# A routing table spread by one-hot products: the scaling moved from VectorE to ScalarE, one turn ahead

## The chip, the cores and the metric

The kernel runs on one core of a Trainium2 chip. Its engines work in parallel, each through its own queue in order: TensorE (PE, with its weight loads as PEld), VectorE (DVE), ScalarE (ACT), GpSimd (POOL) and SyncE (SP), which issues the DMAs. The metric is the device time of one execution in microseconds; the runs of a kernel are given by their median.

## The reference, cut to what matters

The program is a network of two blocks with two layers each, for 256 tokens of 1024 channels. The change sits in the second block, in a feed-forward part that chooses among 16384 experts for each token and head:

```python
s1, s2 = <q1, sub_keys[0]>, <q2, sub_keys[1]>        # 128 + 128 key scores, 8 heads
v1, i1 = top_k(s1, 16);  v2, i2 = top_k(s2, 16)
top_s, pos = top_k(v1[:, None] + v2[None, :], 16)    # 16 of 256 pairs
expert = i1 * 128 + i2 (at pos);  g = softmax(top_s)
w = g * gelu(u_tab[expert] @ h);  y = sum of w * v_tab[expert]
```

Layer 0 does this for 256 tokens and for 256 context tokens, layer 1 for the 256 tokens alone.

## The kernel before

Instead of gathering experts, the kernel computes all of them. `hidden` (L1088) takes one block of 128 experts, loads its weights, cuts them in a high and a low part (`split`: ACT casts the high part on L198, DVE subtracts it on L199), multiplies them with the tokens on PE (three products each, L232 to L234, 48 for 512 tokens, 24 for 256) and applies a gelu on ACT (L1104). `ahead` runs 128 such expert blocks for layer 0 and 126 for layer 1; the result goes to memory. Afterwards `experts` reads it back, weights it with a dense table G of factors [expert, token] and multiplies with the second table.

G is made beside `ahead`, in two steps for each group of 128 tokens. `choose` finds the 16 pairs of each head and leaves a tile R with four columns for each token: first index k0, second index k1, and the factor in a coarse and a fine part, g0 and g1. `spread` turns R into G: per token it makes a one-hot of k0 and two one-hots of k1 scaled by g0 and g1, 128x128 each in 16 bits, for the 128 choices of the token; PE multiplies the first with the second and third and adds up (two products, L1061). Four tokens are one turn: 12 instructions of DVE (L1056 once and L1058 twice for each token), 8 products, one copy from PSUM by ACT (L1062). A group has 32 turns, and after every fourth turn 1 MB of G is stored. The tile E of a turn comes from the tag "wb", a ring of three buffers that weights of other parts use too.

How these steps mix is given by a plan (P0 for layer 0, P1 for layer 1, L39 and L40): pairs of a start and a rate, in units of 256 tokens of expert blocks. Each unit advances each active generator by its rate. In layer 0 a block of 512 tokens counts as two units, and the four spreadings run at 0.8 to 0.95 turns per unit, one after the other, most of the time beside a `choose`. In layer 1 the first spreading runs at 0.5 turns per unit from unit 45 on, the second at 0.85 from unit 85 on, so that for some 25 units both run. The framework then sets the final order of instructions on each engine with its own estimate of their readiness, so that a cast for a later block can stand ahead of a gelu of an earlier one. Two pairs of buffers hold the split weights ("ws", four tiles): a cast for the block after the next can begin when PE has finished the present block.

Below, "block 1" is this stretch of layer 0 (1285 to 1872 us) and "block 2" that of layer 1 (2945 to 3234 us); an "expert block" is one call of `hidden`, and a "turn" is four tokens of a spreading.

Of the kernel before, what the change touches and what calls it, by code (L numbers as in the profile page):

```python
# [12 lines left out]
F16 = mybir.dt.float16  # L13
U32 = mybir.dt.uint32
AF = mybir.ActivationFunctionType
ALU = mybir.AluOpType
AX = mybir.AxisListType

P = 128
# [5 lines left out]
NT = 16  # L25
GSCALE = 2.0 ** 14
# [27 lines left out]
class Net:  # L54
# [989 lines left out]
    def spread(self, r, Gd, nb):  # L1044


        nc = self.nc
        for q in range(P // NT):
            st = self.t("k8", [P, P, NT])
            for m in range(0, NT, 4):  # L1050
                n = q * NT + m
                pG = self.p("C", [P, 4, P])
                E = self.t("wb", [P, 4, 3, P], F16)
                for j in range(4):
                    k0, k1, g0, g1 = (r[:, i, n + j:n + j + 1] for i in range(4))
                    nc.vector.tensor_scalar(E[:, j, 0], self.iota16, k0, None, ALU.is_equal)  # L1056
                    for i, g in enumerate((g0, g1)):
                        nc.vector.tensor_scalar(E[:, j, 1 + i], self.iota16, k1, g, ALU.is_equal, ALU.mult)  # L1058
                for j in range(4):
                    for i in range(2):  # L1060
                        nc.tensor.matmul(pG[:, j], E[:, j, 0], E[:, j, 1 + i], start=i == 0, stop=i == 1)  # L1061
                nc.scalar.activation(st[:, :, m:m + 4], pG.rearrange("p n e -> p e n"), AF.Copy, scale=1 / GSCALE)  # L1062
                if m == NT - 4:
                    nc.sync.dma_start(Gd[:, nb + q], st)
                yield

    def routing(self, l, hs, Gd, order, early, plan):

        ss = [self.t("k8", [P, 16, P]) for _ in range(2 * len(hs))]
        R = {}

        def choose(i):
            R[i] = yield from self.choose(self.rt, ss[i])

        def spread(gen, i, nb):
            self.done(gen)
            yield from self.spread(R[i], Gd, nb)

        gens = [choose(i) for i, _ in order]
        for _ in self.key_scores(l, hs, ss):
            for g in gens[:early]:
                next(g), next(g)
        gens += [spread(g, *o) for g, o in zip(gens, order)]
        return [(t, g, r) for g, (t, r) in zip(gens, plan)]
# [324 lines left out]
```

## Time and profile before

| | us |
|---|---|
| median of 3 runs | 3605.29 (3605.12 to 3605.36) |
| profiled execution | 3616.49 |
| its span | 3614.7 |
| PE busy in the span | 3506.5 (97%) |
| DVE busy | 2563.6 (71%) |
| ACT busy | 1520.0 (42%) |
| L1056 and L1058, DVE | x768 and x1536, mean 246 and 307 ns |

The page gives shares of the whole span; stages differ. A busy PE is not one at its peak, since the ends of matmuls are modelled, so pace is better read from the starts of equal instructions, an expert block's gelu for example. Instructions of ACT and DVE also overlap a little at their ends, so that two in a row take less than twice the duration of one.

### The profile page before, as it was taken

To read this page: it belongs to the slowest core of one execution; us is meant where nothing else is said; L and a number is where in the kernel's file an instruction comes from. 1 tells how busy PE (TensorE), PEld (TensorE's weight loads), DVE (VectorE), ACT (ScalarE), POOL (GpSimd) and SP (SyncE) were. 2 spreads that over 40 slices of the span, in tenths; PEclk is the share of its full clock that TensorE was granted. 3 is DMA by queue.
4 is the path that set the end of the run, shared out by engine and by line. 5 is a ranking of instruction groups with operands and counts; after the bars stand their busy time and mean duration, and the time that the engine had idled before them with its cause. 6 is when DMAs were issued, how large, how long until landed. Compare 5 with 4: busy or idle time off the path is not lost.

```text
span 3614.7 us, 59733 instructions
## 1 busy us (share of the span) xinstructions
PE 3506.5 (97%) x22400; PEld 3053.3 (84%) x22400; DVE 2563.6 (71%) x6767; ACT 1520.0 (42%) x2555; POOL 51.9 (1%) x72
## 2 busy tenths in 40 slices
PE   8999989999999999999999999999999999999999
PEld 6677777899899999998997888888878999888877
DVE  6666776655753799999777655554476789987666
ACT  5533455544553433333333222222254545455443
POOL 1000010000000000000000000000000000000000
PEclk9999999999999999999999999999999999999999
DMA  6555644566522754454579877776223677788986
GB/s 220 168 175 199 209 153 131 184 202 201 167 94 82 223 183 166 163 174 175 181 246 295 263 249 237 236 226 188 76 72 110 214 234 239 240 275 293 291 259 197
DMA packets 329394, 712.85 MB, mean 197 GB/s; under 512 B 28304, under 2 KB 170256, under 8 KB 322704
## 3 DMA queue, kind: packets, MB, share of 16 engines
q1 hardware_dynamic: 329104, 709.05, 60.5%
q8 instruction: 175, 2.87, 0.3%
q14 instruction: 115, 0.94, 0.1%
HBM read 606.44 MB, written 102.50 MB: 196 GB/s over the span
## 4 chain that ended last, share of the span: by engine, by line
PE 67%; DVE 21%; DMA 8%; issue 1%; ACT 1%; SPq 1%; POOL 0%; DVEq 0%; POOLq 0%; ACTq 0%
PE psC L233 9%; PE psC L234 9%; PE psC L232 9%; PE psA L234 8%; PE psA L232 8%; PE psA L233 8%; DVE wb L1058 6%; DVE ws L199 4%; DMA wb<-in_v 3%; DMA k<-kept 3%; PE psB L233 3%; PE psB L232 3%; PE psB L234 3%; DVE wb L1056 2%; DVE k L199 2%; DMA wb<-in_ada_w 1%
## 5 line engine op out<-in xcount | busy, mean ns | idle before, releaser
L198 ACT CAST ws<-w 128x1024 fp32r<-128x1024 f32 (+1 forms) x528 | 547.6, 1037 | 923.5 <-PE psA L233 626.1
L199 DVE TENSOR_TENSOR ws<-w,ws 128x1024 fp32r<-128x1024 f32 (+1 forms) x528 | 635.6, 1205 | 366.4 <-ACT ws L198 360.9
L234 PE MATMUL psA<-b,ws 128*128 128x256 f32 x2760 | 784.2, 284 | 29.3 <-DVE ws L199 28.2
L232 PE MATMUL psA<-b,ws 128*128 128x256 f32 x2760 | 787.4, 285 | 1.1 <-ACT ws L198 1.1
L233 PE MATMUL psA<-b,ws 128*128 128x256 f32 x2760 | 776.6, 281 | 0.0
L234 PEld LDWEIGHTS psA<-b,ws 128*128 128x128 f32 x2760 | 521.8, 189 | 43.7 <-DVE ws L199 43.1
L232 PEld LDWEIGHTS psA<-b,ws 128*128 128x128 f32 x2760 | 522.3, 189 | 7.0 <-ACT ws L198 3.6
L233 PEld LDWEIGHTS psA<-b,ws 128*128 128x128 f32 x2760 | 522.6, 189 | 0.2
L234 PE MATMUL psC<-k,k 128*128 128x512 f32 x1056 | 416.3, 395 | 7.0 <-DVE k L199 6.9
L232 PE MATMUL psC<-k,k 128*128 128x512 f32 x1056 | 417.1, 395 | 6.0 <-ACT k L198 6.0
L233 PE MATMUL psC<-k,k 128*128 128x512 f32 x1056 | 416.4, 394 | 0.0
L1058 DVE TENSOR_SCALAR wb<-iota,R 128x128 f16<-128x128 f16 x1536 | 413.3, 307 | 0.0
L199 DVE TENSOR_TENSOR k<-wb,k 128x1024 fp32r<-128x1024 f32 x256 | 312.4, 1220 | 60.8 <-ACT k L198 60.6
L198 ACT CAST k<-wb 128x1024 fp32r<-128x1024 f32 x256 | 268.4, 1050 | 199.4 <-DMA wb<-in_v 199.1
L198 ACT CAST k<-k 128x256 fp32r<-128x256 f32 (+1 forms) x272 | 137.3, 506 | 484.0 <-PE psA L234 422.6
L1151 DVE TENSOR_TENSOR k<-k,b 128x256 f32<-128x256 f32 x384 | 149.9, 421 | 211.7 <-DMA k<-kept 209.7
L234 PEld LDWEIGHTS psC<-k,k 128*128 128x128 f32 x1056 | 198.5, 188 | 60.3 <-DVE k L199 15.0
L233 PE MATMUL psC<-ws,k 128*128 128x512 f32 (+1 forms) x608 | 240.5, 396 | 5.7 <-DVE ws L199 4.6
L232 PEld LDWEIGHTS psC<-k,k 128*128 128x128 f32 x1056 | 198.9, 188 | 52.6 <-ACT k L198 8.1
L232 PE MATMUL psC<-ws,k 128*128 128x512 f32 (+1 forms) x608 | 239.7, 398 | 0.6 <-ACT k L198 0.2
L234 PE MATMUL psC<-ws,k 128*128 128x512 f32 (+1 forms) x608 | 238.0, 392 | 0.0
L233 PEld LDWEIGHTS psC<-k,k 128*128 128x128 f32 x1056 | 199.0, 188 | 44.2
(400 smaller groups left out, 6250.0 us busy)
## 6 DMA issues: line engine op xcount, KB each, us to landing
w<-in_u SPq DMA_DIRECT2D x256, 512.0 KB, 4.3
wb<-in_v SPq DMA_DIRECT2D x256, 512.0 KB, 4.5
w<-in_w_ff SPq DMA_DIRECT2D x128, 512.0 KB, 4.5
G<-k SPq DMA_DIRECT2D x48, 1024.0 KB, 6.1
b<-G SPq DMA_DIRECT2D x48, 1024.0 KB, 8.5
wb<-in_ada_w SPq DMA_DIRECT2D x80, 512.0 KB, 4.7
k<-kept SPq DMA_DIRECT2D x128, 256.0 KB, 3.8
w<-in_wA SPq DMA_DIRECT2D x48, 512.0 KB, 4.7
```

The costliest lines, as they stand in the source:

```text
L198: self.nc.scalar.copy(hi, src)
L199: self.nc.vector.tensor_sub(lo, src, hi.bitcast(F32))
L232: self.nc.tensor.matmul(out, ah, bh, start=first, stop=False)
L233: self.nc.tensor.matmul(out, ah, bl, start=False, stop=False)
L234: self.nc.tensor.matmul(out, al, bh, start=False, stop=last)
L1056: nc.vector.tensor_scalar(E[:, j, 0], self.iota16, k0, None, ALU.is_equal)
L1058: nc.vector.tensor_scalar(E[:, j, 1 + i], self.iota16, k1, g, ALU.is_equal, ALU.mult)
L1151: nc.vector.tensor_mul(g3, g3, Gs[i][:, :, j])
```

## The change

DVE now writes the two plain one-hots only (L1055 in the new numbering, twice for each token). ACT makes the two scaled ones from the one-hot of k1 (L1057, a copy with a column of R as scale). Both are issued by a helper `ones` for the turn that follows: in each turn the one-hots of the next come first, then this turn's eight products (L1070), its copy (L1071) and the store. The generator has one step more (33 instead of 32), since the first only prepares. The tile E has four planes for each token instead of three; its tag and ring stay. The gelu is now L1114.

```diff
-        for q in range(P // NT):
-            st = self.t("k8", [P, P, NT])
-            for m in range(0, NT, 4):
-                n = q * NT + m
-                pG = self.p("C", [P, 4, P])
-                E = self.t("wb", [P, 4, 3, P], F16)
-                for j in range(4):
-                    k0, k1, g0, g1 = (r[:, i, n + j:n + j + 1] for i in range(4))
-                    nc.vector.tensor_scalar(E[:, j, 0], self.iota16, k0, None, ALU.is_equal)
-                    for i, g in enumerate((g0, g1)):
-                        nc.vector.tensor_scalar(E[:, j, 1 + i], self.iota16, k1, g, ALU.is_equal, ALU.mult)
...
+        def ones(n):
+            E = self.t("wb", [P, 4, 4, P], F16)
+            for j in range(4):
+                col = [r[:, i, n + j:n + j + 1] for i in range(4)]
+                for i in (1, 0):
+                    nc.vector.tensor_scalar(E[:, j, i], self.iota16, col[i], None, ALU.is_equal)
+                for i in (2, 3):
+                    nc.scalar.activation(E[:, j, i], E[:, j, 1], AF.Copy, scale=col[i])
+            return E
+
+        E = ones(0)
+        yield
+        for n in range(0, P, 4):
+            q, m = divmod(n, NT)
+            nxt = ones(n + 4) if n + 4 < P else None
...
+                    nc.tensor.matmul(pG[:, j], E[:, j, 0], E[:, j, 2 + i], start=i == 0, stop=i == 1)
...
+            E = nxt
+            yield
```

On ACT in block 1, one expert block with two turns read before as follows (ws: high part of split weights; psA: an expert block's product, its number a little above that of its ws; psC: a turn's product; k: results).

```order
L1104 ACTIVATE k_2296_13381<-psA_13332 128x512
L1062 ACTIVATE k_2278_13186<-psC_13390 128x128x4
L1062 ACTIVATE k_2301_13420<-psC_13421 128x128x4
L198 CAST ws_13678<-w_13676 128x1024
L1104 ACTIVATE k_2308_13499<-psA_13450 128x512
```

The same place after the change (wb: the tile E of a turn, R: the columns of factors):

```order
L1114 ACTIVATE k_2295_13415<-psA_13366 128x512
L1071 ACTIVATE k_2286_13316<-psC_13441 128x128x4
L1071 ACTIVATE k_2286_13316<-psC_13474 128x128x4
L1057 ACTIVATE wb_13549<-wb_13549,R_12605 128x128 x8
L1057 ACTIVATE wb_13583<-wb_13583,R_12605 128x128 x8
L198 CAST ws_13612<-w_13610 128x1024
L1114 ACTIVATE k_2306_13540<-psA_13491 128x512
```

Sixteen scalings stand between a gelu and the next cast. Before, the cast ahead of the gelu of psA_13450 was that of ws_13678, the second block behind it (13562 is the first); now the cast ahead of the gelu of psA_13491 is that of ws_13612, the first behind it.

On ACT in block 2, where both spreadings run, before:

```order
L1104 ACTIVATE k_4770_32895<-psA_32870 128x256
L1062 ACTIVATE k_4754_32760<-psC_32898 128x128x4
L198 CAST ws_33038<-w_33036 128x1024
L1104 ACTIVATE k_4777_32952<-psA_32927 128x256
L1062 ACTIVATE k_4744_32678<-psC_32955 128x128x4
L198 CAST ws_33120<-w_33118 128x1024
```

And after:

```order
L1114 ACTIVATE k_4741_33290<-psA_33265 128x256
L1057 ACTIVATE wb_33321<-wb_33321,R_32531 128x128 x4
L1071 ACTIVATE k_4728_33187<-psC_33338 128x128x4
L198 CAST ws_33350<-w_33348 128x1024
L1057 ACTIVATE wb_33382<-wb_33382,R_32531 128x128 x8
L1071 ACTIVATE k_4728_33187<-psC_33399 128x128x4
L198 CAST ws_33412<-w_33410 128x1024
L1057 ACTIVATE wb_33444<-wb_33444,R_30373 128x128 x2
L1114 ACTIVATE k_4750_33379<-psA_33354 128x256
```

The cast of ws_33350, for the very next product psA_33354, now stands behind the gelu of psA_33265, the product ahead of it, and behind four scalings and a turn's copy.

On DVE in block 1, around the subtraction of an expert block (iota: the numbers 0 to 127 that the columns of R are compared with), the queue read before:

```order
L1056 TENSOR_SCALAR wb_13538<-iota_223,R_12605 128x128
L1058 TENSOR_SCALAR wb_13538<-iota_223,R_12605 128x128 x2
L199 TENSOR_TENSOR ws_13563<-w_13560,ws_13562 128x1024
L1056 TENSOR_SCALAR wb_13623<-iota_223,R_12605 128x128
L1058 TENSOR_SCALAR wb_13623<-iota_223,R_12605 128x128 x2
```

And after:

```order
L937 MAX_INDEX k_2229_12705<-k_2229_12705,k_2288_13327 128x8
L1055 TENSOR_SCALAR wb_13424<-iota_223,R_12605 128x128 x5
L1055 TENSOR_SCALAR wb_13457<-iota_223,R_12605 128x128 x8
L199 TENSOR_TENSOR ws_13488<-w_13485,ws_13487 128x1024
L935 MATCH_REPLACE k_2296_13418<-k_2229_12705,k_1889_10059 128x128
```

Eight short instructions stand where twelve stood for a turn, and those of the next turn are issued ahead of the subtraction.

## Rows read from the trace of the kernel before

**Rows 1.** Busy time by engine in five stretches: start:end, length, then busy us (instructions) per engine

```profile
1285.00:1419.00 134.00, 127.95 (x1161) 122.97 (x1160) 134.00 (x616) 43.89 (x70) 0.00 (x0) 1.00 0.51 170
1438.00:1716.00 278.00, 261.27 (x2355) 253.67 (x2354) 269.97 (x1187) 96.89 (x151) 0.00 (x0) 0.98 0.50 170
1744.00:1872.00 128.00, 123.21 (x1118) 117.78 (x1117) 111.74 (x402) 47.73 (x72) 0.00 (x0) 1.00 0.64 221
2945.00:3083.00 138.00, 136.37 (x1214) 133.17 (x1213) 135.74 (x483) 70.77 (x113) 0.00 (x0) 1.00 0.75 245
3084.00:3195.00 111.00, 103.07 (x913) 94.52 (x913) 111.00 (x424) 52.90 (x87) 0.00 (x0) 1.00 0.70 237
```

**Rows 2.** The same stretches, casts of L198 alone on ACT: one (x) per expert block

```profile
1285.00:1419.00 134.00, 18.89 (x19) 1.00 0.51 170
1438.00:1716.00 278.00, 40.28 (x39) 0.98 0.50 170
1744.00:1872.00 128.00, 18.52 (x18) 1.00 0.64 221
2945.00:3083.00 138.00, 44.66 (x43) 1.00 0.75 245
3084.00:3195.00 111.00, 27.68 (x27) 1.00 0.70 237
```

**Rows 3.** The same stretches, copies of L1062 alone on ACT: one (x) per turn

```profile
1285.00:1419.00 134.00, 17.78 (x32) 1.00 0.51 170
1438.00:1716.00 278.00, 35.45 (x64) 0.98 0.50 170
1744.00:1872.00 128.00, 17.82 (x32) 1.00 0.64 221
2945.00:3083.00 138.00, 12.91 (x22) 1.00 0.75 245
3084.00:3195.00 111.00, 19.54 (x34) 1.00 0.70 237
```

**Rows 4.** Timeline of ACT, block 1: start us, us, engine, line, operation [idle before]

```profile
1865.66 0.59 ACT L1104 ACTIVATE k<-psA 128x512 f32<-128x512 f32 x1
1866.15 1.07 ACT L1062 ACTIVATE k<-psC 128x512 f32<-128x512 f32 x2
1871.31 1.05 ACT L198 CAST ws<-w 128x1024 fp32r<-128x1024 f32 x1 [4.08 <-PE psA L233]
1872.26 0.59 ACT L1104 ACTIVATE k<-psA 128x512 f32<-128x512 f32 x1
...
1877.89 0.59 ACT L1104 ACTIVATE k<-psA 128x512 f32<-128x512 f32 x1
```

**Rows 5.** Timeline of ACT, block 2, one spreading at work

```profile
3205.51 0.38 ACT L1104 ACTIVATE k<-psA 128x256 f32<-128x256 f32 x1
3205.78 0.59 ACT L1062 ACTIVATE k<-psC 128x512 f32<-128x512 f32 x1
...
3208.88 0.37 ACT L1104 ACTIVATE k<-psA 128x256 f32<-128x256 f32 x1
```

**Rows 6.** Waits in block 1, 1285 to 1872 us: us in total, times, longest

```profile
PE psA L234 <- DVE ws L199: 20.9, 30, 2.3
```

**Rows 7.** Costliest groups of the page: busy us, mean ns; idle before it

```profile
L199 DVE TENSOR_TENSOR ws<-w,ws 128x1024 fp32r<-128x1024 f32 (+1 forms) x528 | 635.6, 1205 | 366.4 <-ACT ws L198 360.9
```

**Rows 8.** Timeline of DVE inside one turn of the spreading

```profile
1380.26 0.24 DVE L1056 TENSOR_SCALAR wb<-iota,R 128x128 f16<-128x128 f16 x1
1380.42 0.52 DVE L1058 TENSOR_SCALAR wb<-iota,R 128x128 f16<-128x128 f16 x2
1380.87 0.24 DVE L1056 TENSOR_SCALAR wb<-iota,R 128x128 f16<-128x128 f16 x1
```

**Rows 9.** ACT's copies by a column of factors, L845: all twenty, ns min/median/max

```profile
L845 ACT ACTIVATE k<-k,rsrf x20: 385/396/489, 950.9 to 2686.0; 128x128 f32<-128x128 f32 x20
```

**Rows 10.** Timeline of ACT: two of those L845 instructions back to back

```profile
2669.48 0.69 ACT L845 ACTIVATE k<-k,rsrf 128x128 f32<-128x128 f32 x2 [0.60 <-DVE k L842]
```

More of the change, by code (lines that the diff above doesn't have):

```diff
@@ L1047, in spread @@
         nc = self.nc
-        for q in range(P // NT):
-            st = self.t("k8", [P, P, NT])
-            for m in range(0, NT, 4):
-                n = q * NT + m
-                pG = self.p("C", [P, 4, P])
-                E = self.t("wb", [P, 4, 3, P], F16)
-                for j in range(4):
-                    k0, k1, g0, g1 = (r[:, i, n + j:n + j + 1] for i in range(4))
-                    nc.vector.tensor_scalar(E[:, j, 0], self.iota16, k0, None, ALU.is_equal)
-                    for i, g in enumerate((g0, g1)):
-                        nc.vector.tensor_scalar(E[:, j, 1 + i], self.iota16, k1, g, ALU.is_equal, ALU.mult)
[L1059 to L1065, printed above, removed]
+        st = None
+        def ones(n):
[12 more added lines that the diff above has]
+            nxt = ones(n + 4) if n + 4 < P else None
+            if m == 0:
+                st = self.t("k8", [P, P, NT])
+            pG = self.p("C", [P, 4, P])
+            for j in range(4):
+                for i in range(2):
+                    nc.tensor.matmul(pG[:, j], E[:, j, 0], E[:, j, 2 + i], start=i == 0, stop=i == 1)
+            nc.scalar.activation(st[:, :, m:m + 4], pG.rearrange("p n e -> p e n"), AF.Copy, scale=1 / GSCALE)
+            if m == NT - 4:
+                nc.sync.dma_start(Gd[:, nb + q], st)
+            E = nxt
+            yield
     def routing(self, l, hs, Gd, order, early, plan):
```

## The prediction, made before the changed kernel ran

> **What bounds the kernel now.** I first read the page's shares by slice: PE is busy nearly throughout, so only the stretches in which it waits can shorten. These are the ones in which the spreading runs. The busy times by engine there [rows 1] are to be read against two counts, the casts of expert blocks [rows 2] and the copies of turns [rows 3]; together they give each engine's load. The first and the last stretch have DVE busy all of their 134 and 111 us, the second 269.97 of 278; PE is not full in any, and ACT has two thirds free in block 1 and half in block 2. The list of waits says what PE lacks: the low part of split weights, which DVE subtracts, 20.9 us in 30 waits in block 1 [rows 6]. So DVE ends last, by its own work, and the change does shorten that work. The question is what ACT's work then does.
>
> PE's own pace comes from gelu starts [rows 4]: 1877.89 less 1872.26 is 5.63 us for an expert block without a turn, 1872.26 less 1865.66 is 6.60 with two, so a turn costs PE 0.485. In block 2 a block has half as many products, 2.82, and with one turn takes 3.37 (3208.88 less 3205.51 [rows 5]): 0.55 for a turn. With 19, 39, 18, 43 and 27 expert blocks and 32, 64, 32, 22 and 34 turns, PE's work in the five stretches is 122.5, 250.6, 116.9, 133.4 and 94.8 us, against 134, 278, 128, 138 and 111 that pass. What PE could win back is thus 11, 27, 11, 5 and 16 us, 70 in all, some 2% of the run.
>
> **What leaves DVE.** A token's three instructions repeat every 0.61 us (1380.87 less 1380.26 [rows 8]); the plain one starts the next 0.16 later, so each scaled one holds the queue for 0.225. A turn is 4 x 0.61 = 2.44 us. After the change it is 8 x 0.16 = 1.28. DVE gives up 1.16 us for each of 192 turns, 223 us; in the fifth stretch its load falls from 111 to about 72, in the second from 270 to 196. DVE is then no one's bound.
>
> **What ACT takes on.** There are 1536 scalings, 8 for each turn. The kernel has the same operation elsewhere, a 128x128 copy with a column as factor: 0.396 us alone [rows 9], and two in a row 0.69 [rows 10], so the second begins 0.295 after the first. I take 0.295, the nearer row, since the eight of a turn stand one behind the other and only the first of each pair waits for DVE; 0.396 is the other end. Below 0.295 lies what the 16-bit tile might save, of which no row speaks. The Trainium skill, page "ScalarE: Activation LUTs", section "What ACT_TABLE_LOAD costs", gives the same rate per element for fp32 and bf16, 93 ns more for each pointer operand, and 93 ns of overlap between neighbours; worked out for 128 columns that is an estimate of 0.386 alone and 0.293 in a row, so by the page nothing is saved by the 16 bits. No run here shows it yet.
>
> The rest of ACT's work in steps from start to start: a cast 0.95 (1872.26 less 1871.31), a gelu 0.49 (1866.15 less 1865.66), a turn's copy 0.48 (two take 1.07 at 0.59 each) [rows 4]; in block 2 a gelu 0.27 [rows 5]. A turn costs ACT 0.48 + 8 x 0.295 = 2.84, an expert block 1.44 in block 1 and 1.22 in block 2. ACT's load becomes 19 x 1.44 + 32 x 2.84 = 118 us in the first stretch, then 238, 117, 115 and 129.5. In block 1 that is PE's own work to within 5% in all three stretches. In the fifth it is 129.5 where 111 pass today: there the wall moves from DVE to ACT and grows by 18.
>
> **How near a stretch comes to its dearest engine.** Before, a stretch with one clear bound reached it fully (first and fifth) or to 97% (second); the third, where DVE is busy for 87% of the time and PE's work is 91% of it, reached neither. After the change block 1 has PE and ACT level, each in order, each waiting for the other. I take 95% there, between the two, 97% for the fourth stretch and 98% for the fifth:
>
> - first: 122.5 / 0.95 = 129, gain 5; second: 250.6 / 0.95 = 264, gain 14; third: 117 / 0.95 = 123, of which I count 2 and not 5, because there the tag "wb" also serves other weights, whose loads start later when a tile E is held a turn longer;
> - fourth: 133.4 / 0.97 = 137.5, nothing;
> - fifth: 129.5 / 0.98 = 132, loss 21;
> - behind it some ten blocks with 0.85 turns each: ACT 1.22 + 0.85 x 2.84 = 3.63 against PE's 2.82 + 0.85 x 0.55 = 3.29 for each, loss 3;
> - one step more for each group: the last gates of layer 1 are stored one block later at most, 2.82 us, and the stage that reads them follows closely; loss 2.
>
> The products (L1070) and stores keep their number, so PE and SP gain and lose nothing in work. Being a turn ahead hides the new hop from DVE to ACT: a turn's chain of 1.28 and 2.4 us fits in the 6 us between its place and that of its products in block 1; without that cover PE would wait some 3 us per block. The sum is -21 in block 1 and +26 in block 2 with its end: +5 us on a profiled execution of 3616.49, which stands 11 above the median of the runs. A few microseconds scale with that by nothing, so the median goes from 3605.29 to **3610 us**. Its own range, for 92 to 97% in block 1, is 3599 to 3623.
>
> **The rivals.**
>
> *The two loads interlock without loss.* Split weights lie two blocks ahead, so ACT may lag in a block with two turns and catch up in one with one. For it speaks that DVE alone managed 100% in two stretches; against it that the new order puts the cast behind sixteen scalings. At 98% in block 1 the gains are 9, 22 and 9, the fourth stretch gives 2, and the fifth, at just ACT's load, loses 18, its end 5: -19, or 3586 us.
>
> *ACT's queue delays the split, slower.* After a gelu, ACT has two copies (0.96) and sixteen scalings (4.72) ahead of the cast; with gelu and cast (0.49 + 0.95) and DVE's subtraction (1.205 [rows 7]) the low part is ready 8.3 us after PE finished a block, while PE reaches the need for it after two turns and one block, 6.6 us. That is 1.7 us late, if nothing catches up. If half of the 76 blocks in the three stretches pay it, 65 us come on top of PE's 490, 555 against today's 540: +15 instead of -21, and with block 2 at +26, +41. It decides from the point where some 30 blocks pay (490 + 30 x 1.7 is today's 540): from there block 1 gives nothing against block 2's loss. I price it a little lower, at +30, 3635 us, because blocks with a single turn recover. Against it speaks that PE's wait also slows what ACT waits for, so that lags do not add up.
>
> A rule points the same way: the Trainium skill, same page, section "Rules for kernel authors", says to use VectorE and not ScalarE for a multiplication. The rows bear it out for a single instruction, 0.225 on DVE against 0.295 on ACT. By that rule alone the change would lose wherever ACT is level with the bound, which is this rival; what speaks for the change is only that DVE was full.
>
> *The scalings do not overlap.* If each holds ACT for 0.396, a turn costs 3.65 and the five stretches 144, 290, 143, 133 and 157 on ACT: +10, +12, +15, 0 and +46, and 8 more behind: some +90, 3695 us. The pair [rows 10] speaks against it.
>
> That the change does less than it says can be excluded: the scaled one-hots are gone from DVE's queue.
>
> **How the numbers follow.** The forecast has 0.44, the interlocked case 0.30, the delayed split 0.20, the scalings without overlap 0.06. Two tenths of a per cent, 7 us, are about what a measurement of this kernel tells from no change. The interlocked case is almost wholly faster, and of the forecast's spread 0.06 lies below 3598 once its tails are counted: 0.36 faster. About half of the forecast's weight, 0.23, is the same; its upper part, 0.15, and the two last cases make 0.41 slower. For 8 in 10 the range goes from 3572, where block 1 gains 35 and block 2 loses little, to 3640, a little over the delayed split.
>
> **What would show it.** Right: L1057 starting every 0.29 to 0.30 us within a turn; DVE's busy time in the first stretch well under 100% and ACT's over 90% in the first, second and fifth; the first three stretches shorter together by about 20 us, the fifth longer by about 20; waits of PE put down to ACT's scaled one-hots and casts instead of the subtraction behind a full DVE. Wrong: the fifth stretch not longer, which would mean that a turn costs ACT less than 2.4 us; or block 1 unchanged with both engines under 90%, which would be the chains and not the loads.

## The result, and the profile after

The changed kernel took 3645.03 us, the median of four runs (3641.28 to 3657.42), against 3605.32 for the kernel before: a ratio of 1.0109, with a 95% interval of 1.0079 to 1.0139. It is slower by 1.1%, where 3610 had been forecast and 3640 was the upper end. The profiled execution took 3646.82 us, 30 more than that of before. Two single runs, one of e4_half below at 7199.55 us and one of the kernel before at 3792.89, lie far above all others of their kernels, and the ratios leave them out.

The page of the kernel after, its span and the engines' busy times:

```profile
span 3645.0 us, 60672 instructions
PE 3524.5 (97%) x22400; PEld 3069.9 (84%) x22400; DVE 2362.5 (65%) x5999; ACT 1960.0 (54%) x4093; POOL 51.9 (1%) x72
```

DVE gave up 201 us and ACT took on 440. PE's busy time grew by 18 us although it has the same 22400 products: some of them ran slower.

To compare stages, each stretch is cut here from the gelu of one expert block to the gelu of the same block in every kernel; the ends thus lie a few microseconds off [rows 1], and the six stretches hold 19, 37, 17, 43, 23 and 14 expert blocks. The kernel before, busy time by engine (columns as in [rows 1]; the three stretches of block 1, then block 2 with one spreading beside a `choose`, with both spreadings, and behind):

```profile
1284.90:1420.20 135.30, 129.25 (x1172) 124.27 (x1171) 135.30 (x624) 44.94 (x71) 0.00 (x0) 1.00 0.51 173
1444.30:1716.50 272.20, 255.48 (x2305) 248.04 (x2304) 264.67 (x1162) 95.00 (x148) 0.00 (x0) 0.98 0.50 170
1749.40:1872.30 122.90, 118.11 (x1072) 112.73 (x1071) 110.95 (x401) 46.78 (x72) 0.00 (x0) 1.00 0.65 224
2948.00:3086.80 138.80, 137.17 (x1231) 134.12 (x1230) 136.54 (x484) 71.76 (x116) 0.00 (x0) 1.00 0.74 243
3086.80:3185.90 99.10, 91.17 (x795) 82.79 (x794) 99.10 (x384) 47.13 (x79) 0.00 (x0) 1.00 0.70 237
3185.90:3230.80 44.90, 44.90 (x417) 44.35 (x415) 37.89 (x121) 23.39 (x39) 0.00 (x0) 1.00 0.83 286
```

The same six stretches of the kernel after:

```profile
1281.20:1411.60 130.40, 125.97 (x1175) 123.70 (x1175) 105.11 (x516) 121.44 (x329) 0.00 (x0) 1.00 0.52 179
1434.30:1697.30 263.00, 251.00 (x2298) 245.26 (x2297) 195.25 (x903) 240.03 (x651) 0.00 (x0) 0.98 0.50 176
1731.70:1865.90 134.20, 123.70 (x1067) 116.77 (x1065) 79.82 (x286) 115.94 (x304) 0.00 (x0) 0.95 0.57 199
2940.10:3074.70 134.60, 133.87 (x1206) 132.03 (x1205) 113.27 (x383) 116.50 (x280) 0.00 (x0) 1.00 0.74 247
3074.70:3212.20 137.50, 116.69 (x820) 102.24 (x818) 72.84 (x288) 119.42 (x330) 0.00 (x0) 0.84 0.50 174
3212.20:3259.80 47.60, 46.34 (x410) 43.98 (x409) 26.35 (x70) 42.61 (x111) 0.00 (x0) 1.00 0.77 260
```

DVE is nowhere full any more. The first two stretches are shorter by 4.9 and 9.2 us, the third longer by 11.4, the fourth shorter by 4.2. The fifth, with both spreadings, has grown from 99.1 to 137.5 us, and there no engine is full: ACT is busy for 87%, PE for 85%, and the granted clock (the first number behind the engines) is 0.84.

The new scalings of the kernel after, all of them (ns min/median/max), and on ACT's timeline eight in a row up to the next instruction, which answer to [rows 9, 10]:

```profile
L1057 ACT ACTIVATE wb<-wb,R x1536: 384/397/440, 1280.6 to 3248.6; 128x128 f16<-128x128 f16 x192
...
1820.15 2.44 ACT L1057 ACTIVATE wb<-wb,R 128x128 f16<-128x128 f16 x8
1822.49 0.58 ACT L1071 ACTIVATE k<-psC 128x512 f32<-128x512 f32 x1
```

One takes 0.397 us, eight take 2.34 from start to start, 0.293 each. The price was right.

The waits in block 1 of the kernel after, 1281 to 1873 us, which answer to [rows 6]:

```profile
DVE ws L199 <- ACT ws L198: 100.6, 38, 7.9
DVE wb L1055 <- PE psC L1070: 60.0, 31, 5.3
ACT ws L198 <- PE psA L233: 57.6, 14, 8.1
PEld psA L232 <- ACT ws L198: 14.0, 13, 2.1
DVE b L766 <- DMA wb<-in_ada_w: 13.9, 7, 4.3
PEld psA L234 <- DVE ws L199: 13.6, 19, 1.6
...
PE psA L232 <- ACT ws L198: 10.5, 11, 1.9
```

PE now waits also for the high part, the cast itself (L232 behind L198), and DVE, with time to spare, waits 60.0 us for PE's products before it may write the next one-hots: the tile that it would write is still being read, so the ring of three is in use.

In the fifth stretch of the kernel after, 3074.7 to 3212.2 us, the three longest:

```profile
DVE wb L1055 <- PE psC L1070: 37.3, 14, 7.8
ACT k L1114 <- PE psA L234: 18.0, 10, 2.6
PEld psA L232 <- ACT ws L198: 15.2, 11, 1.6
```

Here the engine with the largest load, ACT, itself waits 18.0 us for PE's last product of a block, while PE waits for ACT's cast. One turn of that circle, first on ACT's timeline of the kernel after:

```profile
3111.86 0.37 ACT L1114 ACTIVATE k<-psA 128x256 f32<-128x256 f32 x1
3112.12 1.27 ACT L1057 ACTIVATE wb<-wb,R 128x128 f16<-128x128 f16 x4
3113.29 0.58 ACT L1071 ACTIVATE k<-psC 128x512 f32<-128x512 f32 x1
3113.77 1.04 ACT L198 CAST ws<-w 128x1024 fp32r<-128x1024 f32 x1
...
3120.83 0.38 ACT L1114 ACTIVATE k<-psA 128x256 f32<-128x256 f32 x1 [1.66 <-PE psA L234]
```

and on PE's at the same place:

```profile
3111.83 1.83 PE L1070 MATMUL psC<-wb 128*128 128x128 f16 x12
3114.86 0.38 PE L232 MATMUL psA<-b,ws 128*128 128x256 f32 x1 [1.20 <-ACT ws L198]
...
3117.00 0.28 PE L232 MATMUL psA<-b,ws 128*128 128x256 f32 x1
3117.12 0.28 PE L233 MATMUL psA<-b,ws 128*128 128x256 f32 x1
...
3117.61 0.42 PE L233 MATMUL psA<-b,ws 128*128 128x256 f32 x1
3117.82 0.41 PE L234 MATMUL psA<-b,ws 128*128 128x256 f32 x1
```

The cast stands behind four scalings and a copy, so PE waits 1.20 us for it. A little later PE's products start 0.21 us apart instead of 0.12. PE alone in two short windows there (start:end, length, busy, granted clock):

```profile
3114.90:3117.30 2.40, 2.06 (x13) 1.00 0.05 10
3117.40:3120.60 3.20, 3.20 (x17) 0.50 0.92 342
```

The clock falls to 0.50, the lower level (1.2 instead of 2.4 GHz). The block ends late, and ACT stands still for 1.66 us before its gelu; the next casts stand behind that gelu in its queue.

### The profile page after: what moved, and what is told of

It reads as the page before. It is cut to its first block, busy times and chain, and to the rows that moved or that the text cites. A ratio compares the mean times of both kernels' runs of the same rounds, so it can differ in the third digit from the quotient of the medians.

```text
span 3645.0 us, 60672 instructions
## 1 busy us (share of the span) xinstructions
PE 3524.5 (97%) x22400; PEld 3069.9 (84%) x22400; DVE 2362.5 (65%) x5999; ACT 1960.0 (54%) x4093; POOL 51.9 (1%) x72
## 4 chain that ended last, share of the span: by engine, by line
PE 36%; DMA 7%; DVE 5%; ACT 4%; issue 1%; SPq 0%; POOL 0%; DVEq 0%; POOLq 0%; ACTq 0%
PE psA L234 5%; PE psA L232 5%; PE psA L233 5%; PE psC L233 5%; PE psC L234 5%; PE psC L232 5%; DMA k<-kept 3%; DMA wb<-in_v 3%; ACT wb L1057 2%; PE psB L233 2%; PE psB L232 2%; PE psB L234 2%; DVE k L199 2%; DVE ws L199 1%; DVE wb L1055 1%
## 5 line engine op out<-in xcount | busy, mean ns | idle before, releaser
L198 ACT CAST ws<-w 128x1024 fp32r<-128x1024 f32 (+1 forms) x528 | 546.9, 1036 | 597.4 <-PE psA L233 298.4
L232 PE MATMUL psA<-b,ws 128*128 128x256 f32 x2760 | 797.3, 289 | 22.1 <-ACT ws L198 21.9
L234 PE MATMUL psA<-b,ws 128*128 128x256 f32 x2760 | 793.1, 287 | 14.5 <-DVE ws L199 13.0
L233 PE MATMUL psA<-b,ws 128*128 128x256 f32 x2760 | 785.9, 285 | 0.0
L232 PEld LDWEIGHTS psA<-b,ws 128*128 128x128 f32 x2760 | 533.1, 193 | 30.1 <-ACT ws L198 29.3
L234 PEld LDWEIGHTS psA<-b,ws 128*128 128x128 f32 x2760 | 531.8, 193 | 30.0 <-DVE ws L199 29.1
L233 PEld LDWEIGHTS psA<-b,ws 128*128 128x128 f32 x2760 | 533.2, 193 | 0.0
L1057 ACT ACTIVATE wb<-wb,R 128x128 f16<-128x128 f16 x1536 | 476.8, 399 | 16.9 <-DVE wb L1055 13.8
L232 PE MATMUL psC<-k,k 128*128 128x512 f32 x1056 | 416.4, 394 | 5.9 <-ACT k L198 5.8
L198 ACT CAST k<-k 128x256 fp32r<-128x256 f32 (+1 forms) x272 | 137.2, 506 | 490.0 <-PE psA L234 430.0
L198 ACT CAST k<-wb 128x1024 fp32r<-128x1024 f32 x256 | 268.3, 1049 | 188.9 <-DMA wb<-in_v 188.8
L1055 DVE TENSOR_SCALAR wb<-iota,R 128x128 f16<-128x128 f16 x1536 | 275.4, 249 | 118.1 <-PE psC L1070 104.8
L234 PEld LDWEIGHTS psC<-k,k 128*128 128x128 f32 x1056 | 198.5, 188 | 61.9 <-DVE k L199 17.1
L232 PEld LDWEIGHTS psC<-k,k 128*128 128x128 f32 x1056 | 198.6, 188 | 51.8 <-ACT k L198 7.6
L232 PE MATMUL psC<-ws,k 128*128 128x512 f32 (+1 forms) x608 | 239.1, 397 | 1.1 <-ACT ws L198 0.7
```

What stands on the lines that cost most here:

```text
L198: self.nc.scalar.copy(hi, src)
L232: self.nc.tensor.matmul(out, ah, bh, start=first, stop=False)
L233: self.nc.tensor.matmul(out, ah, bl, start=False, stop=False)
L234: self.nc.tensor.matmul(out, al, bh, start=False, stop=last)
L1055: nc.vector.tensor_scalar(E[:, j, i], self.iota16, col[i], None, ALU.is_equal)
L1057: nc.scalar.activation(E[:, j, i], E[:, j, 1], AF.Copy, scale=col[i])
```

## The experiments

Ratios are to the kernel before on the same chip, with 95% intervals. The experiments ran on several chips, on which the median of the kernel before was 3605 to 3613 us, so times of different experiments that lie a few microseconds apart are better compared by their distance to it. Stage times below are from gelu to gelu, as above; "block 1" is here the stretch from 1285 us on with the five blocks that follow the third stretch (1284.9 to 1900.4 us; before 615.5, after 614.1 us), "block 2" the last three stretches together (before 282.9, after 319.7).

### In which layer, and the overlap

**e1_layer0_only**, the new `spread` in layer 0, the old one in layer 1:

```diff
-            yield from self.spread(R[i], Gd, nb)
+            yield from (self.spread_new if l == 0 else self.spread_old)(R[i], Gd, nb)
```

> The new spreading in layer 0 only, the old one in layer 1. Theory 1 (ScalarE is overloaded where both spreadings of layer 1 run): block 2 goes back to its time of before, some 37 us less than the changed kernel; block 1 stays as in the changed kernel, so 3605 to 3610 us. Rival (the new chain costs everywhere, a few us per group): layer 0 has four of the six groups, so two thirds of the 40 us stay, about 3630 us.

Measured 3614.76 us, ratio 1.0008 [0.9999, 1.0018]; block 1 617.1, block 2 283.0. The time is 5 us above the range of theory 1 and far below the rival's. So layer 0 gains nothing, and the loss comes from layer 1.

**e5_apart**, the first spreading of layer 1 at a higher rate, so that it ends before the second begins:

```diff
-P1 = ((5, 0.75), (41, 1.0), (45, 0.5), (85, 0.85))
+P1 = ((5, 0.75), (41, 1.0), (45, 0.85), (85, 0.85))
```

> The changed kernel with one number of layer 1's plan altered: the first spreading runs at 0.85 turns per unit instead of 0.5, so that it ends before the second begins and the two never run together. Theory 1 (ScalarE is the bound where two run): with one spreading a block of 256 tokens costs ScalarE 1.22 + 0.85 x 2.84 = 3.63 us against TensorE's 3.29; 80 blocks are about 290 to 300 us instead of 320, so 20 to 30 us less than the changed kernel. Rival (the new chain costs with every turn, however spread): the same 64 turns, no change beyond 8 us.

Measured 3622.68, ratio 1.0038 [1.0025, 1.0050]; block 2 292.7. The same scalings cost 27 us less when two spreadings don't meet; 10 of the 37 remain.

### Which part of the change

**e2_ahead_only**: the turn ahead stays, DVE scales as before.

```diff
-                for i in (1, 0):
+                for i in (1, 0) if j < 0 else (0,):
                     nc.vector.tensor_scalar(E[:, j, i], self.iota16, col[i], None, ALU.is_equal)
                 for i in (2, 3):
-                    nc.scalar.activation(E[:, j, i], E[:, j, 1], AF.Copy, scale=col[i])
+                    if j < 0:
+                        nc.scalar.activation(E[:, j, i], E[:, j, 1], AF.Copy, scale=col[i])
+                    else:
+                        nc.vector.tensor_scalar(E[:, j, i], self.iota16, col[1], col[i], ALU.is_equal, ALU.mult)
```

(`j < 0` never holds, so no scaling is left on ACT.)

> One turn ahead, but VectorE makes the scaled one-hots itself, as before. Theory 1: the loss is ScalarE's load, so this is within 5 us of the kernel before, 3600 to 3612 us. Rival 2 (a tile held a turn longer in a ring of three buffers makes VectorE wait for TensorE's products): most of the 40 us stay, 3630 us or more, with VectorE waiting for the products for tens of us in block 2.

Measured 3625.13, ratio 1.0042 [1.0027, 1.0056]; block 1 624.7, 9 us more than before. That lies between the two ranges. Being ahead is no free cover; with three tiles it costs by itself (with four it was not run).

**e3_no_ahead**: ScalarE scales all, each turn's tile is made in the turn itself.

```diff
-        E = ones(0)
-        yield
...
-            nxt = ones(n + 4) if n + 4 < P else None
+            E = ones(n)
...
-            E = nxt
```

> ScalarE scales as in the changed kernel, but each turn makes its own one-hots, not a turn ahead. Theory 1: ScalarE's load in the stretch of two spreadings is the same 122 us, so the time stays within 15 us of the changed kernel, 3630 to 3665 us. Rival 2: with tiles held for one turn less the waits for products go and the time falls to 3615 us or under.

Measured 3625.37, ratio 1.0037 [1.0023, 1.0052]; block 1 598.5, 16 us less than with the turn ahead, block 2 315.8. This too lies between the two ranges. The hop from DVE to ACT costs less than its cover does.

**e4_half**, ahead, ScalarE scales two of a turn's four tokens and DVE the other two; **e4_half_look**, the same kernel once more; and **e7_half_no_ahead**, the same split without the turn ahead:

```diff
-                for i in (1, 0):
+                for i in (1, 0) if j < 2 else (0,):
                     nc.vector.tensor_scalar(E[:, j, i], self.iota16, col[i], None, ALU.is_equal)
                 for i in (2, 3):
-                    nc.scalar.activation(E[:, j, i], E[:, j, 1], AF.Copy, scale=col[i])
+                    if j < 2:
+                        nc.scalar.activation(E[:, j, i], E[:, j, 1], AF.Copy, scale=col[i])
+                    else:
+                        nc.vector.tensor_scalar(E[:, j, i], self.iota16, col[1], col[i], ALU.is_equal, ALU.mult)
```

> A turn ahead, ScalarE scales for two of four tokens and VectorE for the other two. A turn then costs ScalarE 0.48 + 4 x 0.295 = 1.66 us and VectorE 2 x 0.61 + 2 x 0.32 = 1.86. Theory 1: in the stretch of two spreadings ScalarE's load falls from 130 to 89 us, VectorE's to 91, both under TensorE's 95, so block 2 gains at least 35 us on the changed kernel and block 1 some 20 to 40: 3570 to 3595 us, below the kernel before. Rival 2 (the tile held longer): 3620 us or more, since it is held as long as in the changed kernel.

> The half version a turn ahead once more, for its profile: 3566 to 3575 us; in the stretch of two spreadings ScalarE and VectorE each under 95% busy and TensorE the fullest, 97 to 102 us for its 23 blocks instead of 137.

> ScalarE scales for two of four tokens, VectorE for two, and each turn makes its own one-hots, not a turn ahead. If being ahead costs by itself (as the two single changes suggest: 15 us with ScalarE's scaling, 9 to 15 without), this is 5 to 15 us below the half version a turn ahead. Rival (with no engine overloaded the lead is free): within 5 us of it.

Measured 3570.71, ratio 0.9883 [0.9867, 0.9900], and again 3566.89, 0.9885 [0.9869, 0.9902]; without the turn ahead 3556.35, 0.9848 [0.9832, 0.9865]. With half of the scalings the same change beats the kernel before. One detail was a miss: in e4_half_look the stretch of two spreadings took 87.0 us and not 97 to 102, and DVE was the fullest there (85.30 us), not PE (83.97). Four stretches of e7_half_no_ahead (the first three and the fifth):

```profile
1281.00:1404.80 123.80, 123.80 (x1175) 123.03 (x1174) 120.58 (x573) 85.59 (x201) 0.00 (x0) 1.00 0.54 190
1428.60:1676.50 247.90, 244.49 (x2292) 240.86 (x2292) 228.73 (x1032) 169.88 (x398) 0.00 (x0) 1.00 0.53 185
1711.00:1828.10 117.10, 114.23 (x1071) 111.81 (x1070) 93.96 (x341) 83.39 (x190) 0.00 (x0) 1.00 0.68 236
3041.60:3125.90 84.30, 83.34 (x802) 80.85 (x800) 84.30 (x333) 80.43 (x203) 0.00 (x0) 1.00 0.79 269
```

PE is full or nearly so in each, at full clock; in the fifth stretch DVE is full as well (84.30 us) and ACT nearly (80.43). By the prediction's prices PE's work for the blocks between these gelus is 122.5, 239.4, 111.2 and 81.9 us (19, 37, 17 and 23 blocks with 32, 64, 32 and 31 turns). The lengths are 1.3, 8.5, 5.9 and 2.4 us above it.

### The third stretch

**e9_ada_later**, the changed kernel with the loads of the modulation weights moved behind block 1; **e12_before_ada_later**, the kernel before with the same edit; **e13_half_ada_later**, e7_half_no_ahead with it:

```diff
-(P0[-1][0], self.ada_rest(MID, 48), 0.3)
+(205, self.ada_rest(MID, 48), 0.8)
```

> The changed kernel with the small modulation weights of layer 1, which share the ring of three buffers with the tiles of the spreading, loaded after the last spreading of layer 0 instead of beside it. Theory (the third stretch lost 11 us because these loads come late in a shared ring): the stretch shortens by 8 to 12 us, about 3635 us. Rival (there ScalarE's load, at 0.95 turns per unit, is the bound): no change beyond 4 us.

> The kernel before, with the modulation weights of layer 1 loaded after the last spreading of layer 0. If these loads hurt only the changed spreading, 104 to 121 stays within 3 us of the 123 us of before and the time with it; if they hurt any spreading through the shared ring or through VectorE's work, it falls by 5 to 10 us.

> The half version, not a turn ahead, with the modulation weights loaded later too. Its third stretch is 117 us where TensorE's work is 111: 3 to 6 us to gain there at most, so 3550 to 3556 us; if TensorE bounds it already, no change.

Measured 3634.35, 1.0075 [1.0058, 1.0092]; 3605.52, 0.9987 [0.9977, 0.9997]; 3557.29, 0.9855 [0.9838, 0.9871]. The third stretch falls from 134.2 to 119.2 after, and from 122.8 to 111.9 before. So most of what these loads cost there they cost in any version; only about 4 of the 15 us belong to the change. In the half version nothing is gained overall: its third stretch falls from 117.0 to 111.9, and the next blocks, which take the loads over, from 28.5 rise to 33.1 us.

### The ring of three tiles

**e10_room_ring3** makes room (four buffers of the tag b8 instead of five) and keeps three tiles, as a control; **e11_room_ring4** uses the room for a fourth:

```diff
-"wb": 3, "b8": 5, "k8": 7, "k4": 4, "k2": 6, "b2": 3
+"wb": 4, "b8": 4, "k8": 7, "k4": 4, "k2": 6, "b2": 3
```

> The changed kernel with four instead of five buffers of the tag b8, and the ring of three as it is: the control of the next. Both theories: within 10 us of the changed kernel, block 1 and block 2 as there.

> The same with a ring of four buffers for the tiles of the spreading instead of three. Theory R (being a turn ahead costs because each tile is held a turn longer in a ring of three): block 1 comes down by the 15 us that lie between the changed kernel and the one not a turn ahead, the third stretch most of all, and the waits of VectorE's one-hots for products shrink by half; some 15 us less than the control. Rival (what costs is the order the scheduler gives, or ScalarE's load): within 5 us of the control.

Measured 3657.42, 1.0130 [1.0111, 1.0148], and 3610.85, 0.9998 [0.9986, 1.0010]. One tile more is worth 47 us, as much as the whole loss, though not in the same places: block 1 falls from 617.8 to 583.7 us, block 2 only from 318.4 to 313.3. Stretches with four tiles (the first three and the fifth):

```profile
1280.10:1407.50 127.40, 125.50 (x1176) 123.57 (x1175) 105.57 (x518) 121.04 (x329) 0.00 (x0) 1.00 0.53 186
1430.20:1681.50 251.30, 246.89 (x2299) 242.83 (x2299) 195.27 (x903) 239.81 (x652) 0.00 (x0) 0.99 0.52 183
1715.60:1837.10 121.50, 116.40 (x1087) 113.16 (x1086) 77.30 (x275) 111.06 (x296) 0.00 (x0) 1.00 0.67 231
3047.30:3177.50 130.20, 110.54 (x820) 96.35 (x818) 72.79 (x288) 116.94 (x322) 0.00 (x0) 0.88 0.53 183
```

and the waits in block 1, 1280 to 1865 us:

```profile
DVE ws L199 <- ACT ws L198: 90.7, 52, 4.4
ACT ws L198 <- PE psA L233: 59.1, 16, 4.2
DVE wb L1055 <- PE psC L1070: 47.6, 26, 4.0
...
PEld psA L234 <- DVE ws L199: 10.6, 17, 1.6
...
PEld psA L232 <- ACT ws L198: 1.8, 3, 0.8
...
PE psA L232 <- ACT ws L198: 1.3, 2, 0.7
```

PE's waits for the cast fall from 14.0 and 10.5 us (weight loads and products) to 1.8 and 1.3, and DVE's longest wait for a cast from 7.9 to 4.4 us. DVE's waits for products fall only from 60.0 to 47.6 us, where theory R had expected half; so the gain is seen at the casts, and how it comes from the ring is not shown step by step. Part of it is PE's clock: in the third stretch it was granted at 0.95 with three tiles and at 1.00 with four. The fifth stretch keeps 31 of its 38 us.

Is this the change's own loss, or would any version gain? **e14_before_ring4** is the kernel before with four tiles, **e15_no_ahead_ring4** e3_no_ahead with four, **e16_half_no_ahead_ring4** and **e17_half_ahead_ring4** the two half versions with four; the edit is the same line.

> The kernel before with a ring of four tiles 'wb' (b8 4 for the room). Theory R, that the ring costs only where tiles are held across the hop to ScalarE and a turn longer: before, L1056 waits only 8.6 us in all for PE's products, so 3595 to 3612, no change of more than 10 us. Rival W, that a fourth tile speeds up any version (the modulation weights and the one-hots share it): 3555 to 3580.

> ScalarE scales all, not a turn ahead, ring of four. With a ring of three this took 3625. Theory R: not ahead, a tile is held only over the hop and the products; the one-hots waited 82.8 us for products with three tiles, so some 15 to 30 us come back: 3595 to 3612, as the version ahead with four tiles (3611). Rival: the ring bites only together with being ahead: 3618 to 3630.

> ScalarE scales two tokens of four, not ahead, ring of four. With three tiles 3556; the one-hots waited only 24.6 us for products. Theory R: 3546 to 3558, at most 10 us to gain. Rival W: 3510 to 3535.

> ScalarE scales two tokens of four, a turn ahead, ring of four. With three tiles 3567. Theory R, that all that being ahead loses is the missing tile: equal to the version not ahead with four tiles within 5 us, 3545 to 3558. Rival O, that being ahead loses by the order in which casts stand behind scalings, whatever the ring: 3560 to 3572, 10 us above the version not ahead.

| kernel | three tiles | its ratio | four tiles | its ratio |
|---|---|---|---|---|
| before (same chip) | 3611.20 | 1 | 3603.87 | 0.9984 [0.9974, 0.9993] |
| all on ScalarE, ahead | 3645.03 | 1.0109 [1.0079, 1.0139] | 3610.85 | 0.9998 [0.9986, 1.0010] |
| all, not ahead | 3625.37 | 1.0037 [1.0023, 1.0052] | 3602.88 | 0.9976 [0.9963, 0.9988] |
| half, ahead | 3566.89 | 0.9885 [0.9869, 0.9902] | 3562.82 | 0.9863 [0.9846, 0.9879] |
| half, not ahead | 3556.35 | 0.9848 [0.9832, 0.9865] | 3551.11 | 0.9822 [0.9805, 0.9838] |

By the ratios the fourth tile is worth 6 us to the kernel before, and 8 and 9 to the half versions, hardly more. Where all scalings go to ACT it is worth 40 us ahead (47 against the control) and 22 not ahead. So most of the ring's price is a cost of the change (R, not W), and not of being ahead alone. Being ahead still costs 8 us with all scalings on ACT and four tiles, and in the half versions 11 to 12 us whatever the ring, as rival O had it. The last line is the fastest of all versions.

### PE's clock in the fifth stretch

**e18_more_products**: in layer 1, eight products of constants ahead of each turn's own, written over by them:

```diff
+            for j in range(8):
+                nc.tensor.matmul(pG[:, j % 4], self.iota16, self.iota16, start=True, stop=True)
             for j in range(4):
                 for i in range(2):
```

> The changed kernel, with eight products of two constants added on TensorE in each turn of layer 1, ahead of the turn's own products and written over by them; nothing else needs them. They are some 17 us of PE work for the 31 turns of the overlap, which took 137.5 us there at a granted clock of 0.84 with ScalarE busy for 87%. Theory C, that the excess over ScalarE's load comes from PE's clock falling while it waits for the casts: the granted clock of the overlap rises to 0.93 or more, and the overlap gets shorter in spite of more work, 115 to 132 us; the run 3620 to 3642. Rival L, that ScalarE's queue alone sets the pace: 136 to 142 us there, the run 3642 to 3655. Rival P, PE's own work: 150 to 160 us there, the run 3660 or more.

Measured 3651.85, ratio 1.0109 [1.0093, 1.0126]. The fourth to sixth stretch:

```profile
2944.60:3087.10 142.50, 142.19 (x1362) 140.68 (x1361) 115.20 (x384) 117.53 (x277) 0.00 (x0) 1.00 0.70 233
3087.10:3213.10 126.00, 116.83 (x1109) 105.58 (x1106) 71.25 (x287) 119.25 (x332) 0.00 (x0) 0.96 0.55 191
3213.10:3262.20 49.10, 49.06 (x472) 47.78 (x470) 26.33 (x70) 43.45 (x111) 0.00 (x0) 1.00 0.79 259
```

With nearly 300 products more, the fifth stretch is 11.5 us shorter, its clock 0.96, and ACT is busy for 95% of it: theory C for this stretch. The list of its waits says the same, ACT's wait for PE's last product falls from 18.0 to 6.6 us:

```profile
ACT k L1149 <- PE psA L234: 6.6, 7, 1.8
```

The time of the run was a miss and lies in rival L's range: the fourth stretch, where PE is full, pays 8 us for the same products, and the saving is gone. One thing is not separated from the clock: the order on ACT changed a little too, in places a gelu stands one scaling earlier.

**e19_no_overlap_ring4**: e11_room_ring4 with the third entry of P1 at 0.85.

> The changed kernel with a ring of four tiles and the two spreadings of layer 1 kept apart (third entry of P1 at 0.85 instead of 0.5). Each alone took 45 and 22 us off. If they act in different stretches they add up: 3580 to 3592. Rival, that both take off the same waits: 3600 to 3611.

Measured 3586.82, ratio 0.9923 [0.9907, 0.9940]. The two repairs add up: 24 us come off in block 2 (313.3 to 289.0), as many as 3610.85 less 3586.82. With all scalings on ACT this is the best that was found, still 36 us behind the half version.

## Why the prediction was wrong

The forecast was -21 us in block 1 and +26 in block 2 with its end; measured from gelu to gelu, block 1 changed by -1.4 and block 2 by +36.8. So 20 us were missed in block 1 and 11 in block 2.

| stretch | before | forecast | after | after, four tiles |
|---|---|---|---|---|
| first | 135.3 | -5 | 130.4 (-4.9) | 127.4 (-7.9) |
| second | 272.2 | -14 | 263.0 (-9.2) | 251.3 (-20.9) |
| third | 122.8 | -2 | 134.2 (+11.4) | 121.5 (-1.3) |
| fourth | 138.8 | 0 | 134.6 (-4.2) | 135.4 (-3.4) |
| fifth | 99.1 | +21 | 137.5 (+38.4) | 130.2 (+31.1) |
| behind it | 45.0 | +3 | 47.6 (+2.6) | 47.6 (+2.6) |

- *The prices of instructions were right.* 0.295 us for a scaling was measured as 0.293, and ACT's load in the second stretch, forecast at 238, was 240.03. DVE gave up somewhat less than forecast, 69.4 us of 74 there (264.67 to 195.25) and 201 of 223 in all. The Trainium skill, page "ScalarE: Activation LUTs", section "What ACT_TABLE_LOAD costs", led to estimates of 0.386 alone and 0.293 in a row; the trace, with 0.397 and 0.293, agrees, and the 16 bits saved nothing (0.396 in [rows 9] for 32 bits).
- *The step that failed first: "Being a turn ahead hides the new hop ... fits".* It was checked against time (1.28 and 2.4 us in 6) and not against the ring. A tile that waits for ACT's scalings, and a turn longer, is one of three; with four the run is 47 us shorter than its control, with none ahead 20 us shorter than the change. The prediction had counted 3 us for this, in the third stretch alone ("I count 2 and not 5"); in block 1 the fourth tile is worth 30 (614.1 to 583.7, the control had 617.8), and not being ahead 16 (to 598.5). That the first stretch came out at its forecast of -5 is partly luck, since the ring's loss is in it. The case "ACT's queue delays the split" named the place, PE's wait for the cast behind scalings, and a price of +30 near the measured +40, but put it on ACT's queue alone and not on the ring.
- *The step that failed second: "98%" for the fifth stretch.* The load was right: for the 23 blocks and 31 turns between these gelus the prediction's prices give 23 x 1.22 + 31 x 2.84 = 116 us, and ACT is busy for 119.42. But that is 87% of the stretch. The forecast took PE's 2.82 us for a block as given, at full clock. PE, waiting for casts, ran part of the time at 0.50; blocks came late to ACT's gelu, and the engine that should have been full stood still. With PE kept busier the stretch takes 126.0, of which ACT's 119.25 are 95%. So of the 38.4 us some 11.5 go with the clock (137.5 less 126.0, although the added products cost PE time of their own), 20 with ACT's load (119.25 less 99.1), and 7 were not divided further. The ring's part, 7 us by the fourth tile, lies within these.
- *"95%" for block 1* was fair where the ring allows it: with four tiles PE's work (122.5, 239.4 and 111.2 us for these blocks) is 96, 95 and 92% of the three lengths.
- *One count was wrong.* In its second stretch the prediction took 39 casts for 39 blocks; from 1438.37 to 1716.49 us there are 38 gelus, since ACT casts ahead. PE's work there was 245 us and not 250.6, and the gain at 95% would have been 20 and not 14. With that the forecast for block 1 is -27, and the miss there 26 us; the four tiles' -20.9 for the second stretch agrees with it.
- *The reading of before was right:* DVE was the bound, and with half of the scalings off DVE every stretch comes near PE's own work. What the prediction didn't ask was whether all of the work has to move. A turn of half the scalings costs ACT 0.48 + 4 x 0.293 = 1.65 us and DVE 4 x 0.16 + 2 x 0.16 + 4 x 0.225 = 1.86; for the 23 blocks and 31 turns of the fifth stretch that is an estimate of 23 x 1.22 + 31 x 1.65 = 79 us on ACT and 31 x 1.86 + 23 x 1.205 = 85 on DVE (1.205 for a subtraction [rows 7]), with PE at 82. It took 84.3, with ACT busy for 80.43 and DVE for all of it.

The Trainium skill, page "ScalarE: Activation LUTs", section "Rules for kernel authors", prefers VectorE for a multiplication; the trace bears it out for one instruction (0.225 us on DVE, 0.293 on ACT) and for the move of all, and the half version shows its limit: with VectorE full, ScalarE's slower instruction is the cheaper one.

Left open: whether three tiles cost by the wait itself or by the order that the framework makes of it, since with a fourth tile the order of casts and scalings on ACT changes too. Why the half versions lose 11 us by being ahead was not taken further than that the ring isn't the reason; why the version with DVE's own scaling loses by it is open as well.

## What to carry to other kernels

Move work off a full engine only until both are level: here half of the scalings took 1.2% off, all of them cost 1.1%, with nothing else altered. In this kernel working a turn ahead across two engines wanted a buffer for the turn, so count the ring's tiles against those in use before counting the time that is hidden. Where an engine that is nearly full releases PE, ask what PE's clock does when it waits, since here it turned the wait into a second one.

## What was not expected of the hardware

PE's short waits were dear: after a wait of 1.20 us for a cast, at 3114.86 us, products at 0.12 us were followed by 3.2 us at a granted clock of 0.50 with products 0.21 apart. Over the fifth stretch the clock was 0.84, and PE was busy for 116.69 us with the work for which the half version takes 83.34. Eight small products more for each turn brought the clock to 0.96 and the stretch from 137.5 to 126.0 us: there more work on an engine made a stage shorter.
